# A DeltaNet and neighbourhood-attention layer: attention with unnormalised probabilities, a negated maximum, and norms of two chunks at a time

## The chip, the core and the metric

The kernel runs on one core of one Trainium2 chip. The core has five engines with a queue each: TensorE (PE, matmuls; its weight loads are listed as PEld), VectorE (DVE), ScalarE (ACT), GpSimd (POOL) and SyncE (SP, which issues the DMAs here). Each works through its queue in the order in which the program was laid out, and waits on semaphores of the others. The metric is the device time of one execution in microseconds (us), the median of the runs.

## What is computed

The layer takes 1024 latent tokens and 256 context tokens of width 1024. Half of the mixing width is a gated DeltaNet (a scan over chunks, forward and backward), half is attention: 8 heads of width 64, each latent query with one softmax over a window of latent keys and all context keys. Then come an output projection, a gated residual and a SwiGLU feed-forward part. What the change touches, cut to the core:

```python
# attention, per row block (s_win: scores of the window plus bias; s_ctx: scores of the context keys)
s = jnp.concatenate([s_win.reshape(B, H, N_COL_BLK, QB_W, n_win), s_ctx], axis=-1)
p = jax.nn.softmax(s, axis=-1).astype(v.dtype)
o = (jnp.einsum("bhnqic,binchd->bnqhd", p_win, v_r)
     + jnp.einsum("bhnqk,bkhd->bnqhd", p[..., n_win:], v_ctx))
# DeltaNet, end: sum of both directions, RMS norm per head, output gate
o = (o_f + rev(o_b)).transpose(0, 2, 1, 3)
o = rms_norm(o, out_norm_w) * jax.nn.silu(z.astype(jnp.float32))
```

## The kernel before

The kernel is one long program in stages. Input projections, short convolutions and the chunks' inverses come first. Then comes the stage of this case, in which the DeltaNet scan and the attention run side by side; after it the output projection and the feed-forward part, both almost pure matmul.

*The scan.* Ten chunks of 128 tokens (two of context, eight latent) are scanned in both directions; step `i` of the loop over `NCH` takes the i-th chunk of each direction. `scan(d, c)` is a generator: up to its first `yield` it multiplies keys by the state (L1106) and forms `vn` on DVE (L1108), then queries by the state (L1116), `y` by `vn` (L1125), the scaling `vk` on ACT (L1129), then `at` by `vn` into `oacc` (L1137, L1138) and the new state (L1142, L1148). A latent chunk that both directions have passed is finished: `finish(c)` squares it on ACT (L1163), forms an inverse root with `rsqrt`, eleven dependent steps of DVE on 128x4 numbers (L182 to L187) with three small ones around it (L1165, L1166, L1168), multiplies by it and by the gate `z` (L1170), transposes on PE (L1175) and splits the result in two parts for the output projection (L1178, L1179). From step 6 on each step finishes two chunks, one of each direction.

*The attention.* `pair(...)` handles 128 queries of two heads (`u` = 0, 1); there are 32 pairs. For each head PE forms 640 scores per query (L296) into a PSUM tile `sc` of 1536 columns, of which there are two (`bufs=2`): 640 columns for each head, and the rest, up to 1408, for the output. DVE adds the bias tile `bt` and takes the maximum in one instruction (L298, two rows in the profile: the operation and the readout of its accumulator), negates it (L300); ACT forms the exponential and its sum (L301); DVE forms the reciprocal of the sum (L302) and multiplies the 640 probabilities by it (L303). After a `yield`, PE transposes the probabilities in five blocks per head (L308), back into `sc`, and ACT copies them to `pt` (L311). After another `yield`, PE multiplies by the values (L318); the two heads use 64 columns of the array each and lie side by side. ACT copies the result into the output tile `no` (L320), and `sc` is free for the next pair but one.

*The order.* The attention is a generator too (`fill`). After each piece of the scan, `beside(PACE)` adds 0.72 to a counter, and each whole number in it advances the attention by one piece. The framework then lays the instructions of each engine out by priority and readiness, so the order in a queue isn't that of the code alone.

## Time and profile before

| what | value |
|---|---|
| median of 3 runs | 1564.35 us (1562.84 to 1565.23) |
| profiled execution | 1570.02 us, span 1568.2 us |
| mean granted TensorE clock | 0.979 |
| PE, weight loads, DVE, ACT, POOL busy | 1473.0, 1228.2, 1000.3, 721.1, 185.6 us |
| stage with scan and attention, 570 to 825 us: PE, DVE, ACT busy | 225.57, 191.87, 160.28 us of 255 |
| DMA share in this stretch | 0.78, 238 GB/s |

Busy time is a share of a stretch of time in which an engine had an instruction in work; matmuls overlap each other, so a busy PE can still have holes. In the groups by line, `x64 | 35.5, 554 | 0.5` means 64 instructions, 35.5 us busy, 554 ns each on average, and 0.5 us in which the engine was idle just before them, followed by what ended that. A 32-bit matmul shows up as two records of PE.

### The profile page before, as it was taken

Reading aid. Unit: us, or ns where it says so; the run is one execution under the profiler, and the core shown is the slowest. Engines: PE = TensorE matmul, PEld = TensorE weight load, DVE = VectorE, ACT = ScalarE, POOL = GpSimd, SP = SyncE. Lnnn points to the kernel's source line nnn. Section 1 sums busy time; section 2 is a strip of 40 time slices with the busy share of each in tenths; the row PEclk is TensorE's granted clock in tenths of the full one; section 3 lists DMA queues with packets and bytes.
Section 4 is the critical chain, followed back from the end, with each engine's and each line's share of the span. In section 5 each row is a group of like instructions: output and inputs, shape, how many; then the busy total and the mean of one; then the engine's idle time right before and its main releaser. Section 6 shows DMA issues by size and latency. Waiting matters only on the chain.

```text
span 1568.2 us, 23886 instructions
## 1 busy us (share of the span) xinstructions
PE 1473.0 (94%) x8535; PEld 1228.2 (78%) x8535; DVE 1000.3 (64%) x1877; ACT 721.1 (46%) x1406; POOL 185.6 (12%) x253
## 2 busy tenths in 40 slices
PE   3999998999999989899979989999999999999999
PEld 1789777777988868787867878888888888888887
DVE  4866479345264665678986469855555556689642
ACT  5443262684356345566753265333333334445441
POOL 1043710342043300000000000000000000000000
PEclk9999899999999999999998999999999999999999
DMA  9457133654468489899639402533323224698742
GB/s 368 132 191 229 46 85 114 218 166 144 155 217 248 154 226 307 262 287 280 199 97 303 177 29 78 194 108 116 101 101 101 101 101 146 222 369 308 236 153 82
DMA packets 214503, 280.50 MB, mean 179 GB/s; under 512 B 16288, under 2 KB 120304, under 8 KB 213360
## 3 DMA queue, kind: packets, MB, share of 16 engines
q1 hardware_dynamic: 213520, 278.34, 54.4%
q8 instruction: 67, 1.10, 0.3%
q10 hardware_dynamic: 864, 0.63, 0.1%
q14 instruction: 52, 0.43, 0.1%
HBM read 212.02 MB, written 71.08 MB: 181 GB/s over the span
## 4 chain that ended last, share of the span: by engine, by line
PE 67%; ACT 4%; DMA 4%; DVE 3%; issue 2%; POOL 1%; SPq 1%; DVEq 0%; POOLq 0%; ACTq 0%
PE ps L1232 27%; PE ps L1579 13%; PE blk L390 6%; PE ps L1363 4%; PE blk L581 3%; PE sc L318 2%; PE sc L308 2%; PE sc L296 2%; PE pr L929 2%; PE ps L1125 1%; PE ps L1385 1%; PE pr L920 1%; PE ps L1137 1%; PE ps L1142 1%; PE ps L1106 1%
## 5 line engine op out<-in xcount | busy, mean ns | idle before, releaser
L390 PE MATMUL blk<-hh,whi 128*128 128x512 f32 (+1 forms) x416 | 125.5, 396 | 9.9 <-ACT zt L592 5.7
L1293 ACT CAST uhi<-ws 128x512 fp32r<-128x512 f32 x91 | 54.8, 624 | 150.0 <-PE ps L1232 71.3
L1293 ACT CAST uhi<-wq 128x512 fp32r<-128x512 f32 x101 | 60.7, 622 | 135.6 <-issue 61.3
L390 PE MATMUL blk<-hh,wlo 128*128 128x512 f32 (+1 forms) x416 | 117.7, 379 | 2.3 <-POOL wlo L200 2.3
L390 PE MATMUL blk<-hl,whi 128*128 128x512 f32 (+1 forms) x416 | 116.4, 378 | 0.0
L1294 DVE TENSOR_TENSOR ulo<-wq,uhi 128x512 fp32r<-128x512 f32 x101 | 67.4, 688 | 66.1 <-ACT uhi L1293 36.0
L1232 PE MATMUL ps<-hT,uhi 128*128 128x512 f32 x336 | 104.6, 392 | 3.2 <-ACT hT L1411 3.1
L1232 PE MATMUL ps<-lT,uhi 128*128 128x512 f32 x336 | 103.8, 390 | 0.0
L1232 PE MATMUL ps<-hT,ulo 128*128 128x512 f32 x336 | 103.4, 389 | 0.0
L390 PEld LDWEIGHTS blk<-hh,whi 128*128 128x128 f32 x416 | 70.4, 195 | 25.6 <-ACT zt L592 6.0
L1232 PE MATMUL ps<-hB,uhi 128*128 128x512 f32 x288 | 89.7, 392 | 0.0
L390 PEld LDWEIGHTS blk<-hh,wlo 128*128 128x128 f32 x416 | 74.4, 195 | 19.3 <-POOL wlo L200 2.8
L1232 PE MATMUL ps<-lB,uhi 128*128 128x512 f32 x288 | 89.3, 391 | 0.0
L1232 PE MATMUL ps<-hB,ulo 128*128 128x512 f32 x288 | 88.8, 389 | 0.0
L581 PE MATMUL blk<-zhi,hh 128*128 128x264 f32 (+1 forms) x288 | 85.3, 296 | 0.0
L390 PEld LDWEIGHTS blk<-hl,whi 128*128 128x128 f32 x416 | 74.2, 194 | 14.1
L1294 DVE TENSOR_TENSOR ulo<-ws,uhi 128x512 fp32r<-128x512 f32 x91 | 60.8, 687 | 36.1 <-ACT uhi L1293 27.8
L581 PE MATMUL blk<-zhi,hl 128*128 128x264 f32 (+1 forms) x288 | 82.8, 287 | 0.0
L581 PE MATMUL blk<-zlo,hh 128*128 128x264 f32 (+1 forms) x288 | 82.4, 286 | 0.0
L1232 PEld LDWEIGHTS ps<-hT,uhi 128*128 128x128 f32 x336 | 63.1, 189 | 16.9 <-ACT hT L1411 3.5
L1232 PEld LDWEIGHTS ps<-lT,uhi 128*128 128x128 f32 x336 | 63.4, 189 | 13.3
L1232 PEld LDWEIGHTS ps<-hT,ulo 128*128 128x128 f32 x336 | 63.2, 188 | 13.2
(331 smaller groups left out, 3555.0 us busy)
## 6 DMA issues: line engine op xcount, KB each, us to landing
wq<-w_fo SPq DMA_DIRECT2D x99, 256.0 KB
wq<-w_gu SPq DMA_DIRECT2D x88, 256.0 KB
wad<-wa SPq DMA_DIRECT2D x64, 256.0 KB
bt<-rpb SPq DMA_DIRECT2D x64, 192.0 KB
t_d<-g SPq DMA_DIRECT2D x22, 512.0 KB
fr<-t_d SPq DMA_DIRECT2D x44, 256.0 KB
f_d<-g SPq DMA_DIRECT2D x33, 256.0 KB
fr<-f_d SPq DMA_DIRECT2D x33, 256.0 KB
```

Source lines behind the costliest of these rows:

```text
L296: pe.matmul(sc[:, u * 640 + n0:u * 640 + n1], q, ks[i], start=i == 0, stop=i == 1)
L308: pe.transpose(sc[:, u * 640 + j * 128:u * 640 + (j + 1) * 128], bt[:, j * 128:(j + 1) * 128], ident)
L318: pe.matmul(sc[u * ND:u * ND + ND, 1280:1408], vv, pt[:, j * 128:(j + 1) * 128], start=j == 0, stop=j == 4)
L390: pe.matmul(o, ww[:, k], xx[k][:, s], start=k == 0 and j == 0, stop=k == KT - 1 and j == end)
L581: pe.matmul(p[:, :c1 - c0], x[k][:, s], ww[:, k, c0:c1], start=k == 0 and j == 0, stop=k == KT - 1 and j == 2)
L920: pe.matmul(p[:, h * 128:h * 128 + 96], kk[:, h], fx[:, h, s], start=True, stop=True)
L929: pe.matmul(p[q, h * 128:h * 128 + 32 * r], f[:, h, q], y[:, h, s], start=True, stop=True)
L1232: pe.matmul(o, w[wi][:, k], x[xi][:, k], start=first and k == 0 and j == 0, stop=k == n - 1 and j == 2, skip_group_check=True)
L1293: act.copy(hi, self.raw[key])
L1294: dve.tensor_tensor(lo, self.raw[key], hi.bitcast(F32), OP.subtract)
L1363: pe.matmul(o, w[wi][:, k], parts[xi][k][:, s], start=k == 0 and j == 0, stop=k == KT - 1 and j == 2)
L1579: pe.matmul(o[b], w[wi][:, b], F[xn, p][xi], start=n in (0, 1, 5) and p == 0 and j == 0, stop=p == NFB // 2 - 1 and j == 2, skip_group_che ...
```

## The change

Four edits, all in this stage:

- The instruction at L298 now forms minus the biased score and its minimum, which is the negated maximum; the exponential takes its input times -1. The separate negation goes.
- The probabilities stay unnormalised. One reciprocal of both heads' sums (`mx[:, :, 1:2]`) replaces two, and the multiplication of the 640 probabilities goes. After the value products, two more matmuls per pair (identity times the reciprocals, repeated over 64 columns, L319 of the changed kernel) put each query's reciprocal into all 64 rows of its head, in columns 1408 to 1536 of `sc`; ACT copies them to a tile `rb` (L322) in place of its copy of the output, and DVE multiplies the output by them into `no` (L323).
- `finish` takes a list of chunks: the squares of both, one `rsqrt` on 128x8 numbers, then the rest for both.
- `finish` is no longer part of a direction's scan: chunks that end are gathered in `ended`, and a generator of its own runs for them, whose pieces advance the attention by two paces.

Lines of the changed kernel from L300 on differ from those of the kernel before: transposes L306, value products L316, norms L1170 to L1178.

On DVE, in the stretch from step 7 to step 8 of the scan, this stood in a row before (`vn` belongs to the scan):

```order
L298 ISA bt,mx<-sc,bt 128x640
L298 ISA mx 128x1
L300 TENSOR_SCALAR mx<-mx 128x1
L302 RECIPROCAL mx<-mx 128x1
L303 TENSOR_SCALAR bt<-bt,mx 128x640
L1108 SCALAR_TENSOR_TENSOR vn<-ps,EG,v 128x128 x2
L302 RECIPROCAL mx<-mx 128x1
L1108 SCALAR_TENSOR_TENSOR vn<-ps,EG,v 128x128
L303 TENSOR_SCALAR bt<-bt,mx 128x640
```

and now, at the last `vn` of the scan:

```order
L298 ISA bt,mx<-sc,bt 128x640
L298 ISA mx 128x1
L1112 SCALAR_TENSOR_TENSOR vn<-ps,EG,v 128x128 x4
L302 RECIPROCAL mx<-mx 128x2
L1112 SCALAR_TENSOR_TENSOR vn<-ps,EG,v 128x128
L323 TENSOR_TENSOR no<-sc,rb 128x8x16
```

The long multiplications and the negations are gone from between the scan's `vn`; one reciprocal and the output's multiplication, which waits for ACT, stand there instead.

On PE, behind a pair's value products, after the first half of a finish; before (`cst` is the identity, so L308 are transposes):

```order
L318 MATMUL sc<-pt,vw 64x128 x4
L318 MATMUL sc<-pt,vc 64x128
L318 MATMUL sc<-pt,vw 64x128
L318 MATMUL sc<-pt,vc 64x128
L308 MATMUL sc<-cst,bt 128x128 x5
L296 LDWEIGHTS qs
L296 MATMUL sc<-kh,qs 128x256
```

and now:

```order
L316 MATMUL sc<-pt,vw 64x128
L316 MATMUL sc<-pt,vc 64x128
L319 MATMUL sc<-cst,mx 64x128 x2
L306 MATMUL sc<-cst,bt 128x128 x5
L1185 MATMUL ps<-cst,oacc 128x128 x4
L306 MATMUL sc<-cst,bt 128x128 x5
L1185 MATMUL ps<-cst,oacc 128x128 x4
L296 LDWEIGHTS qs
```

Before, the next scores (L296) came right behind five transposes; now the two spreading matmuls follow the products, and all ten transposes and the scan's own stand before the next scores.

On DVE, the norms at the end of the stage; before (part of it):

```order
L185 TENSOR_TENSOR nwt<-orr 128x4
L1165 TENSOR_TENSOR orr<-orr,RQ_110 128x4
L186 SCALAR_TENSOR_TENSOR nwt<-nwt 128x4
L1166 TENSOR_SCALAR nwt<-orr 128x4
L187 SCALAR_TENSOR_TENSOR orr<-nwt,orr 128x4
L182 TENSOR_SCALAR nwt<-nwt 128x4
```

and now:

```order
L1170 TENSOR_TENSOR orr<-orr,RQ_110 128x4 x2
L1173 TENSOR_SCALAR nwt<-orr 128x8
L182 TENSOR_SCALAR nwt<-nwt 128x8
L183 TENSOR_SCALAR orr<-nwt 128x8
L185 TENSOR_TENSOR nwt<-orr 128x8
L186 SCALAR_TENSOR_TENSOR nwt<-nwt 128x8
L187 SCALAR_TENSOR_TENSOR orr<-nwt,orr 128x8
```

Two chunks' steps took turns; now there is one row of steps, of which each needs the one before it.

```diff
--- before.py
+++ after.py
@@ -295,13 +295,11 @@
                     for i in range(2):
                         pe.matmul(sc[:, u * 640 + n0:u * 640 + n1], q, ks[i], start=i == 0, stop=i == 1)
                 m = mx[:, u]
-                dve.tensor_tensor_reduce(bt, sc[:, u * 640:u * 640 + 640], bt, 1.0, -3.0e38, OP.add, OP.max,
+                dve.tensor_tensor_reduce(bt, sc[:, u * 640:u * 640 + 640], bt, -1.0, 3.0e38, OP.add, OP.min,
                                          m[:, 0:1])
-                dve.tensor_scalar(m[:, 1:2], m[:, 0:1], -1.0, None, op0=OP.mult)
-                act.activation(bt, bt, AF.Exp, bias=m[:, 1:2], accum_out=m[:, 2:3])
-                dve.reciprocal(m[:, 3:4], m[:, 2:3])
-                dve.tensor_scalar(bt, bt, m[:, 3:4], None, op0=OP.mult)
+                act.activation(bt, bt, AF.Exp, bias=m[:, 0:1], scale=-1.0, accum_out=m[:, 1:2])
             yield 1
+            dve.reciprocal(mx[:, :, 2:3], mx[:, :, 1:2])
             pts = []
             for u, bt in enumerate(bts):
                 for j in range(5):
@@ -317,8 +315,14 @@
                     vv = (vals[j] if w0 else vals[(j + 2) % 5])[:, u * ND:u * ND + ND]
                     pe.matmul(sc[u * ND:u * ND + ND, 1280:1408], vv, pt[:, j * 128:(j + 1) * 128],
                               start=j == 0, stop=j == 4)
-            act.copy(out.rearrange("p (r b c) -> p r b c", r=8, b=4)[:, :, cb],
-                     sc[:, 1280:1408].rearrange("p (r c) -> p r c", r=8))
+            for u in range(2):
+                pe.matmul(sc[u * ND:u * ND + ND, 1408:1536], mx[:, u, 2:3].to_broadcast([128, ND]), ident,
+                          start=True, stop=True)
+            rb = nw.tile([128, 128], F32, name="rb", tag="rb")
+            act.copy(rb, sc[:, 1408:1536])
+            dve.tensor_tensor(out.rearrange("p (r b c) -> p r b c", r=8, b=4)[:, :, cb],
+                              sc[:, 1280:1408].rearrange("p (r c) -> p r c", r=8),
+                              rb.rearrange("p (r c) -> p r c", r=8), OP.mult)
             yield 1
 
         order = [(hp, half, cb) for hp in range(NAH // 2) for half in range(2) for cb in range(4)]
@@ -1151,35 +1155,42 @@
             yield 1
             if lat:
                 if c in seen:
-                    yield from finish(c)
+                    ended.append(c)
                 seen.add(c)
 
-        def finish(c):
-            o = oacc[:, c - 2]
-            z, sq = work("z"), work("sq", 1)
-            sp.dma_start(fl(z), z_d[(c - 2) * 128:(c - 1) * 128])
-            r = sw.tile([128, 4], F32, name="orr", tag="orr")
-            for h in range(4):
-                act.activation(sq[:, h], o[:, h], AF.Square, accum_out=r[:, h:h + 1])
-            t = sw.tile([128, 3, 4], F32, name="nwt", tag="nwt")
-            dve.tensor_tensor(r, r, RQ2[:, c - 2], OP.mult)
-            dve.tensor_scalar(t[:, 0], r, 1.0 / DH, EPS, op0=OP.mult, op1=OP.add)
-            rsqrt(r, t[:, 0], t[:, 1])
-            dve.tensor_tensor(r, r, RQ[:, c - 2], OP.mult)
-            for h in range(4):
-                dve.scalar_tensor_tensor(o[:, h], o[:, h], r[:, h:h + 1], z[:, h], op0=OP.mult, op1=OP.mult)
-            yield 1
-            yield 1
-            p = bank()
-            for h in range(4):
-                pe.transpose(p[:, hs[h]], o[:, h], ident)
-            hi, lo = (x[:, :, (c - 2) * 128:(c - 1) * 128] for x in ga)
-            p = p.rearrange("p (h i) -> p h i", h=4)
-            act.activation(hi, p, AF.Copy, scale=onw)
-            dve.scalar_tensor_tensor(lo, p, onw, hi.bitcast(F32), op0=OP.mult, op1=OP.subtract)
-            yield 1
+        def finish(cs):
+            zs = []
+            r = sw.tile([128, 2, 4], F32, name="orr", tag="orr")
+            for i, c in enumerate(cs):
+                z, sq = work("z"), work("sq", 1)
+                sp.dma_start(fl(z), z_d[(c - 2) * 128:(c - 1) * 128])
+                zs.append(z)
+                for h in range(4):
+                    act.activation(sq[:, h], oacc[:, c - 2, h], AF.Square, accum_out=r[:, i, h:h + 1])
+                dve.tensor_tensor(r[:, i], r[:, i], RQ2[:, c - 2], OP.mult)
+            t = sw.tile([128, 2, 8], F32, name="nwt", tag="nwt")
+            r8 = r.rearrange("p i h -> p (i h)")
+            dve.tensor_scalar(t[:, 0], r8, 1.0 / DH, EPS, op0=OP.mult, op1=OP.add)
+            rsqrt(r8, t[:, 0], t[:, 1])
+            for i, c in enumerate(cs):
+                dve.tensor_tensor(r[:, i], r[:, i], RQ[:, c - 2], OP.mult)
+                for h in range(4):
+                    dve.scalar_tensor_tensor(oacc[:, c - 2, h], oacc[:, c - 2, h], r[:, i, h:h + 1], zs[i][:, h],
+                                             op0=OP.mult, op1=OP.mult)
+            yield 2
+            yield 2
+            for c in cs:
+                p = bank()
+                for h in range(4):
+                    pe.transpose(p[:, hs[h]], oacc[:, c - 2, h], ident)
+                hi, lo = (x[:, :, (c - 2) * 128:(c - 1) * 128] for x in ga)
+                p = p.rearrange("p (h i) -> p h i", h=4)
+                act.activation(hi, p, AF.Copy, scale=onw)
+                dve.scalar_tensor_tensor(lo, p, onw, hi.bitcast(F32), op0=OP.mult, op1=OP.subtract)
+            yield 2
 
         last = [ORDER[0][-1], ORDER[1][-1]]
+        ended = []
         count = [0.0]
 
         def beside(n):
@@ -1197,10 +1208,16 @@
             live = [scan(d, ORDER[d][i]) for d in range(2)]
             while live:
                 nxt = []
-                for n, g in enumerate(live):
-                    if next(g, 0):
+                for g in live:
+                    n = next(g, 0)
+                    if n:
                         nxt.append(g)
-                    beside(PACE)
+                    beside(PACE * max(n, 1))
+                if ended:
+                    g = finish(ended[:])
+                    ended.clear()
+                    beside(PACE * next(g))
+                    nxt.append(g)
                 live = nxt
         for _ in fill:
             pass
```

## The prediction

> **What bounds the kernel now.** I read the page first (engines, then the chain that ended last), then cut the stage that the change touches into stretches of time, then read single groups and the queue of VectorE.
>
> ```profile
> PE 1473.0 (94%) x8535; PEld 1228.2 (78%) x8535; DVE 1000.3 (64%) x1877; ACT 721.1 (46%) x1406; POOL 185.6 (12%) x253
> PE 67%; ACT 4%; DMA 4%; DVE 3%; issue 2%; POOL 1%; SPq 1%; DVEq 0%; POOLq 0%; ACTq 0%
> ```
>
> TensorE (PE) is busy for 94% of the span and carries 67% of the chain that ended last; VectorE (DVE) carries 3%. So DVE work is worth something only in a stretch where it starves PE. The change touches only the stage in which the DeltaNet scan and the attention run side by side, about 570 to 824 us. This table cuts it by what runs there; the columns are length, then busy time and instruction count of PE, weight loads, DVE, ACT and POOL, then granted clock, DMA share and GB/s.
>
> ```profile
> 590.00:613.00 23.00, 21.18 (x186) 18.66 (x182) 12.13 (x41) 12.83 (x46) 0.62 (x2) 1.00 1.05 342
> 613.00:648.00 35.00, 30.55 (x278) 25.93 (x278) 22.31 (x72) 22.01 (x54) 3.65 (x11) 0.95 0.79 247
> 648.00:670.00 22.00, 21.53 (x204) 19.09 (x203) 15.84 (x50) 14.02 (x37) 1.87 (x6) 1.00 0.91 276
> 670.00:691.00 21.00, 20.79 (x198) 18.43 (x196) 15.43 (x50) 13.28 (x36) 1.56 (x5) 1.00 0.90 274
> 691.00:713.00 22.00, 20.37 (x195) 18.09 (x195) 16.91 (x57) 11.86 (x31) 2.22 (x6) 1.00 0.99 294
> 713.00:735.00 22.00, 19.24 (x173) 16.23 (x174) 18.36 (x79) 13.85 (x41) 1.87 (x6) 0.92 0.94 277
> 735.00:748.00 13.00, 12.15 (x122) 10.84 (x122) 11.29 (x38) 8.39 (x21) 1.25 (x4) 1.00 0.91 277
> 750.00:767.00 17.00, 15.14 (x135) 11.91 (x136) 16.24 (x74) 11.86 (x35) 1.87 (x6) 1.00 0.70 209
> 767.00:781.00 14.00, 13.99 (x145) 12.41 (x146) 12.79 (x43) 9.94 (x26) 1.72 (x4) 1.00 0.59 184
> 783.00:799.00 16.00, 14.22 (x129) 11.28 (x127) 15.46 (x70) 11.07 (x32) 1.87 (x6) 1.00 0.47 147
> 799.00:810.00 11.00, 10.92 (x111) 9.75 (x110) 9.90 (x36) 6.38 (x14) 0.00 (x0) 1.00 0.08 24
> ```
>
> The recorded busy time of PE contains the latency of each matmul, so I count matmul records per us instead. Three kinds of stretch show. (1) Up to 713, the two long even stretches (648 to 691) run 402 records in 43 us, 9.3 per us, with DVE at 73% and DMA at 0.9; before them, 613 to 648 runs 7.9 per us with DVE at 64%: DVE isn't what is short there. (2) The stretches 713-735, 750-767 and 783-799, in which finished chunks are normalised (I call them the finish stretches), run 437 records in 55 us, 7.9 per us, with DVE busy for 50.06 of 55 us (91%). (3) The stretches between them, 735-748, 767-781 and 799-810, run 378 records in 38 us, 9.95 per us. So PE is starved by DVE in 55 us of the kernel, and nowhere else for long.
>
> **The change part by part.**
>
> ```profile
> L298 DVE CUSTOM_DVE_ANT_0 bt<-sc,bt 128x640 f32<-128x640 f32 x64 | 52.5, 822 | 22.6 <-PE sc L296 10.7 <-POOL bt L264 4.6 <-DMA bt<-rpb 3.7
> L303 DVE TENSOR_SCALAR bt<-bt,mx 128x640 f32<-128x640 f32 x64 | 35.5, 554 | 0.5
> L302 DVE RECIPROCAL mx<-mx 128x1 f32<-128x1 f32 x64 | 10.2, 159 | 8.8 <-ACT bt L301 8.1
> L300 DVE TENSOR_SCALAR mx<-mx 128x1 f32<-128x1 f32 x64 | 9.2, 147 | 0.5
> L1131 DVE TENSOR_TENSOR vn<-ps,NB 128x512 f32<-128x512 f32 x16 | 11.0, 688 | 5.5 <-ACT vk L1129 5.0 <-PE ps L1125 0.3
> L185 DVE TENSOR_TENSOR nwt<-orr 128x4 f32<-128x4 f32 x24 | 3.8, 158 | 0.1
> L320 ACT COPY no<-sc 128x128 f32<-128x128 f32 x32 | 8.5, 266 | 16.3 <-PE sc L318 16.0
> 772.23 1.24 PE sc L318 x20
> 713.00:735.00 22.00, 2.87 (x6) 0.92 0.94 277
> 750.00:767.00 17.00, 2.75 (x5) 1.00 0.70 209
> 783.00:799.00 16.00, 2.38 (x5) 1.00 0.47 147
> ```
>
> The last three rows are the stretches again, with only the probabilities' multiplication (L303) counted.
>
> *DVE, per pair of heads.* Removed: two multiplications, two reciprocals, two negations, 2 x (0.554 + 0.159 + 0.147) = 1.72 us. Added: one reciprocal of two columns, 0.16 us by L302, and one multiplication of 128x128 from PSUM: between L185 (4 columns, 0.158) and L1131 (512 columns, 0.688) a straight line gives 0.29. Net 1.27 us less; over 32 pairs 41 us of DVE. The finish stretches hold 16 such multiplications, 8 pairs, so 10 us of their 50.
>
> *ACT.* The exponential takes a constant factor and the same bias, and the copy of the output becomes an equal copy of the spread reciprocals: 0.266 us out, 0.266 in. Nothing.
>
> *PE.* Two matmuls per pair are added, in the same shape and the same side-by-side placing as the value products. Those are 20 records in 1.24 us (the row above, from the chain), 0.062 each; the two new ones make 4 records, 0.25 us. Over 32 pairs 8 us. Nothing hides work of PE where PE is the bound. The bounds are 0.25 us a pair and nothing (a pair in a hole of PE).
>
> *The finish stretches.* If DVE isn't short any more, PE can run their 437 records at the neighbours' 9.95 per us: 43.9 us, and 8 x 0.25 = 2.0 for the new matmuls, 45.9 instead of 55. DVE would need 50 - 10 = 40 us there, so PE sets it. That is -9.1 at best; at worst nothing, if ACT holds PE instead. I take -7.5, near the upper end, because the neighbours reach their rate with DVE still 89% busy. One of these stretches also holds a half clock:
>
> ```profile
> 725.70:729.10 3.40, 3.27 (x20) 2.94 (x22) 2.88 (x21) 1.98 (x5) 0.62 (x2) 0.50 0.83 197
> ```
>
> It follows a hole of PE behind DVE and costs about 1.7 us of the 9.1.
>
> *The rest after 713* (38 us, 7 pairs): 7 x 0.25 = +1.75 of PE at worst, nothing at best; DVE gets shorter by 8.9 of 34 us. I take +1.
>
> *Before 713* (33 multiplications of the 64, 16.5 pairs): +4.1 if all of it shows. In 590 to 648 the DMA share (1.05) and the low rate leave holes for half of it, and each head's chain of scores, maximum, exponential, transposes loses the negation, the reciprocal and the multiplication, 0.86 us, ahead of the transposes, which also frees the bias buffers earlier. Bounds -3 and +4.1; I take +0.5.
>
> *The score buffer.* Two buffers of scores exist. Before, the buffer went free after the value products and a 0.266 us copy; now after the products, the spread, the copy, a hop to DVE and 0.29 us. The order of PE allows for it: before, in 15 of 32 pairs at most the five transposes of one head stood between a pair's last product and the next scores on PE; now in 6. Each of these 6 would wait about 0.4 us longer (0.29, and 0.1 that I allow for the hop), +2.4; against that the waits of before go:
>
> ```profile
> PE sc L296 <- ACT no L320: 2.0, 6, 0.4
> ```
>
> I take +0.5, bounds -2 and +4. Behind the waiting scores stand the scan's matmuls on PE, so such a wait delays both.
>
> *The norms of two chunks in one.* Here the count of instructions misleads. These are the norms at the end of the stage, first one chunk alone, then both mixed:
>
> ```profile
> 814.97 0.16 DVE L1165 TENSOR_TENSOR orr<-orr,RQ 128x4 f32<-128x4 f32 x1 [0.45 <-ACT sq L1163]
> 815.17 0.17 DVE L1166 TENSOR_SCALAR nwt<-orr 128x4 f32<-128x4 f32 x1
> ...
> 816.45 0.15 DVE L1165 TENSOR_TENSOR orr<-orr,RQ 128x4 f32<-128x4 f32 x1
> 816.57 0.16 DVE L186 SCALAR_TENSOR_TENSOR nwt<-nwt 128x4 f32<-128x4 f32 x1
> 816.65 0.16 DVE L1166 TENSOR_SCALAR nwt<-orr 128x4 f32<-128x4 f32 x1
> ...
> 820.17 1.14 DVE L1170 SCALAR_TENSOR_TENSOR oacc<-oacc,orr,z 128x128 f32<-128x128 f32 x4
> ...
> 820.67 1.17 PE L1175 MATMUL ps<-cst,oacc 128*128 128x128 f32 x4 [1.25 <-DVE oacc L1170]
> ```
>
> A step that needs the one before it starts 0.20 us after it; steps of two chunks in turn start 0.10 apart. Twice twelve steps in turn take 2.4 us, and twelve merged steps that wait for each other take 2.4 too. So I price the merge at 0 (best: -1.2 per finish, where other work of DVE fills the gaps). At the end of the stage it is no gain: now all eight multiplications wait for the second chunk's squares; from 816.45 come 0.2 for that step, 2.4, 0.3 for two small products and eight multiplications at 1.14 for four, so the last one ends near 821.6, where before it ended at 821.3. I take +0.3 (bounds -1.2 and +1.5).
>
> The Trainium skill, page "VectorE: DVE Perf Modes", section "Rules for kernel authors", says that chained operations gain nothing from tricks between them and that only the count of operations matters. By that rule a merge would save 12 x 0.16 = 1.9 us each of the four times, 7.7 in all, and the sum would be near 1551; the rows above go against it where two chains alternate.
>
> *Sum*: -7.5 + 1 + 0.5 + 0.5 + 0 + 0.3 = -5.2 us. The profiled execution took 1570.02 us (span 1568.2); the sum makes it 1564.8. The median of the runs is 1564.35, 0.36% below the profiled one; the same 5.2 us from it give 1559.2.
>
> **The rivals.**
>
> *More than that.* DVE relief shows everywhere: the finish stretches give all 9.1, the rest after 713 gives 1 instead of costing 1, the part before 713 gives 2, the release costs nothing, the tail gives 1.2: -13.3, 1551. For it: DVE is 89% busy in the stretches between, too. Against: they run at the highest rate of the stage already.
>
> *No change.* PE pays for what DVE gains. ACT has 36.8 us in the 55 us of the finish stretches, and the largest waits of PE in the stage are for ACT's copies of the transposed probabilities, which the change keeps:
>
> ```profile
> PEld sc L318 <- ACT pt L311: 7.2, 18, 1.1
> PEld sc L308 <- ACT pt L311: 5.7, 13, 1.5
> ```
>
> If these hold half of the finish stretches' gain, 3.7 us, the sum is -1.5: 1562.9.
>
> *Slower.* The output's multiplication stands in DVE's queue behind a maximum of the next pair (0.822 and its 0.08 readout) that was issued earlier; the scores of the pair after next wait for it on PE, with the scan behind them. If that happens, a release comes 0.4 + 0.9 = 1.3 us late. It decides where less than that stands between: about 12 pairs, 12 x 0.9 = +10.8 in place of my +0.5, sum +5: 1569.5. Against: the order of PE was laid out around it. That it happens in fewer than 6 pairs would make it harmless. The Trainium skill, page "PSUM — Partial Sum Buffer", section "Engine vs sequencer instructions", calls these queues strictly first in, first out, which speaks for this rival; no row of before shows this multiplication.
>
> **How the numbers follow.** Chances: my forecast (2 to 9 us gained) 0.47, more than that 0.13, no change 0.23, slower 0.17. A measurement of this kernel tells about 0.2%, 3.1 us, from no change. Faster by more: 0.13 and nearly all of the forecast's, 0.42, together 0.55; within: 0.23 and the rest of the forecast, 0.28; slower 0.17. The range goes from 1551 (the first rival) to 1569 (just short of the last); the forecast alone would be 1555 to 1562.
>
> **What would show it.** Right: the finish stretches get shorter by 6 to 8 us together at 9.5 or more records per us; DVE falls by about 40 us in the stage; the new matmuls take 0.25 us a pair; the last transposes of the stage come no earlier behind the end of the scan than now. Wrong: PE waits for the output's multiplication with more than 4 us in total (the slower rival); the finish stretches keep their length while PE waits for the copies L311 (no change); the part before 713 moves by more than 4 us either way, since there I only guess how holes and added matmuls meet.

## The result, and the profile after

The changed kernel takes 1567.76 us (median of 11 runs) where the kernel before, in the same job, takes 1564.35 us: a ratio of 1.0027, 95% interval 1.0015 to 1.0040. A second job, reported below, gave 1.0008 (0.9996 to 1.0021). So the change costs about 1 or about 4 us, by the job; the second can't be told from no change by itself. The prediction was 1559.2 us, a gain of 5.2.

The page of the profiled execution (1565.93 us), its busy times and the shares of the chain that ended last:

```profile
PE 1478.5 (95%) x8663; PEld 1233.2 (79%) x8663; DVE 968.6 (62%) x1701; ACT 721.1 (46%) x1406; POOL 185.4 (12%) x253
PE 75%; DMA 10%; ACT 5%; DVE 4%; POOL 3%; issue 2%; SPq 1%; ACTq 0%; POOLq 0%; DVEq 0%
```

DVE has 32 us less, PE 128 matmul records more, ACT the same. This single profile is 4 us shorter than the one that the prediction started from, against the medians; so both kernels were profiled again, and the stage is read from these. Four stretches each, cut at the scan's matmuls `at` x `vn` (L1137 before, L1141 after): from the first scores to the first of them (step 2), to step 6 (the first step that finishes chunks), to the last step, and to the first matmul of the output projection. Columns as in the prediction's table. The kernel before, profiled again:

```profile
573.90:613.70 39.80, 31.82 (x264) 26.73 (x263) 22.34 (x66) 24.26 (x64) 1.87 (x6) 0.91 0.95 296
613.70:710.30 96.60, 91.95 (x870) 80.56 (x869) 70.73 (x230) 61.34 (x157) 9.28 (x28) 1.00 0.92 278
710.30:806.60 96.30, 88.89 (x842) 75.32 (x842) 87.10 (x341) 64.48 (x174) 8.57 (x26) 1.00 0.67 199
806.60:819.60 13.00, 5.73 (x46) 4.31 (x45) 9.34 (x41) 5.49 (x22) 0.00 (x0) 0.81 0.31 109
```

The changed kernel, first profile:

```profile
573.20:614.90 41.70, 34.55 (x281) 28.65 (x281) 19.51 (x53) 25.43 (x67) 1.87 (x6) 0.92 0.91 281
614.90:711.40 96.50, 95.38 (x917) 83.30 (x916) 57.11 (x169) 60.95 (x153) 8.74 (x28) 1.00 0.93 277
711.40:809.90 98.50, 95.35 (x926) 80.29 (x925) 73.45 (x250) 64.68 (x177) 8.12 (x26) 1.00 0.69 200
809.90:821.50 11.60, 4.23 (x24) 3.27 (x25) 8.11 (x29) 4.76 (x20) 0.00 (x0) 0.67 0.29 94
```

And its second profile:

```profile
572.10:616.10 44.00, 35.89 (x281) 30.28 (x281) 19.52 (x53) 25.49 (x67) 1.87 (x6) 0.88 0.84 265
616.10:713.10 97.00, 95.37 (x918) 83.37 (x917) 57.12 (x169) 60.93 (x154) 8.72 (x28) 1.00 0.94 278
713.10:811.50 98.40, 95.25 (x925) 80.28 (x924) 73.40 (x250) 64.58 (x177) 8.09 (x26) 1.00 0.67 198
811.50:823.20 11.70, 4.32 (x25) 3.37 (x25) 8.16 (x29) 4.82 (x20) 0.00 (x0) 0.70 0.29 98
```

The stage takes 245.7 us before, 248.3 and 251.1 after: +1.9 and +4.2 ahead of step 2 (the second profile has one half clock more there, a piece of time with a granted clock of 0.50, 3.4 us long), -0.1 and +0.4 up to step 6, +2.2 and +2.1 in the steps that finish chunks, -1.4 and -1.3 at the end. The third stretch holds 84 records of PE more, about 60 of the spreading and some 20 that stood in the fourth before, so the last two are best read together: +0.8 both times. The place where the prediction saw its gain has not become shorter, although DVE fell from 87.1 of 96.3 us (90%) to 73.45 of 98.5 (75%).

The first profile of before, from which the prediction argued, had a stage of 250.1 us. The 4.4 us more lie at two places, each with a half clock that the second profile doesn't have: step 2 to 3 took 35.5 us there and 31.8 here, step 6 to 7 35.4 and 34.2. The latter is the half clock from which the prediction took 1.7 of its 9.1 us.

What the two new operations cost on PE can be read at any pair that has no wait behind it. Before, the last value product and what follows on PE:

```profile
796.48 0.27 PE L318 MATMUL sc<-pt,vc 128*64 128x128 f32 x1
796.68 0.94 PE L1106 MATMUL ps<-s,kT 128*128 128x128 f32 x6
```

After, with the copy on ACT and the multiplication on DVE:

```profile
802.39 0.27 PE L316 MATMUL sc<-pt,vc 128*64 128x128 f32 x1
802.50 0.39 PE L319 MATMUL sc<-cst,mx 128*64 128x128 f32 x4
802.82 0.77 PE L306 MATMUL sc<-cst,bt 128*128 128x128 f32 x5
...
802.93 0.27 ACT L322 COPY rb<-sc 128x128 f32<-128x128 f32 x1 [0.49 <-PE sc L319]
...
803.23 0.29 DVE L323 TENSOR_TENSOR no<-sc,rb 128x128 f32<-128x128 f32 x1 [0.34 <-ACT rb L322]
```

From the last product's start to the next operation 0.20 us before and 0.43 after; over all 32 pairs the medians are 0.20 and 0.42. So the spreading costs PE 0.22 us a pair, 7.0 us in all. The score buffer goes free 1.07 us behind the last product here (from 802.39, plus 0.06 for the product itself, to 803.52); the mean over the 32 pairs is 1.48 us, before it was 0.77. The multiplication itself takes 0.29 us, as priced.

### The profile page after: what moved, and what is told of

It reads as the page before. It is cut to its first block, busy times and chain, and to the rows that moved or that the text cites. A ratio compares the mean times of both kernels' runs of the same rounds, so it can differ in the third digit from the quotient of the medians.

```text
span 1564.2 us, 23860 instructions
## 1 busy us (share of the span) xinstructions
PE 1478.5 (95%) x8663; PEld 1233.2 (79%) x8663; DVE 968.6 (62%) x1701; ACT 721.1 (46%) x1406; POOL 185.4 (12%) x253
## 4 chain that ended last, share of the span: by engine, by line
PE 75%; DMA 10%; ACT 5%; DVE 4%; POOL 3%; issue 2%; SPq 1%; ACTq 0%; POOLq 0%; DVEq 0%
PE ps L1249 26%; PE ps L1596 13%; PE blk L394 11%; PE ps L1380 4%; PE sc L316 3%; PE blk L585 2%; PE sc L306 2%; PE sc L296 2%; PE pr L933 2%; DMA nv_d<-zt 1%; DMA wraw<-w_conv 1%; PE ps L1129 1%; PE ps L1110 1%; PE pr L924 1%; PE ps L1146 1%
```

## The experiments

All ratios are to the kernel before in the same job; five rounds each (9 to 12 runs, where nothing else is said).

**Both kernels once more**, to know what one profile is worth.

> The kernel before, once more, as a yardstick. Its profiled execution took 1570.02 us, 5.7 over the median of its runs, and its stage (first scores L296 to first L1363) 250.1 us, 1.8 more than the 248.3 of the changed kernel, which by its runs is 4.2 us slower. If that one profile was an outlier, the stage takes 243 to 247 us here and the ratio is within 0.15% of 1. If the loss of the change lies outside the stage, the stage takes 250 again.

Ratio 1.0002 (0.9987 to 1.0017), stage 245.7 us: the first profile of before was the outlier.

> The changed kernel, once more. The first profile's stage took 248.3 us. If the loss of 0.27% lies in the stage, the stage takes 248 to 251 us here and stays at least 2 us above that of the kernel before in the same job; if it lies elsewhere, the two stages are alike or this one is shorter, and the loss shows as half clocks in the 740 us behind it. Ratio 1.001 to 1.004 by either.

1.0008 (0.9996 to 1.0021), stage 251.1 us. Both profiles say that what the change costs lies in the stage: outside it they are 1.5 and 2.1 us shorter than the second one of before.

**Each half of the change alone.** The attention's edits with the old `finish`, and the merged `finish` with the old attention; each is one part of the diff above, unchanged.

> The attention's edits alone (negated maximum in one step, unnormalised probabilities, spread reciprocals, output multiplied on DVE); the norms as before. Theory 1 (PE pays 0.25 us a pair for the spreading and DVE's relief buys nothing back, because the scan's chain of dependent steps, not DVE, sets the finish stretches): +4 to +8 us, ratio 1.002 to 1.005. Theory 2 (the loss comes from the merged finish, which gives the attention 15 paces a step where it had 14 and leaves the end of the stage without cover): -2 to -6 us, ratio 0.996 to 0.999. The prediction's terms without the merge: -5.5 us.

1.0032 (1.0018 to 1.0047), +5.0 us, the worst of the three. Its profile, the four stretches:

```profile
569.90:611.60 41.70, 33.55 (x280) 27.76 (x280) 19.43 (x53) 25.25 (x67) 1.87 (x6) 0.96 0.90 282
611.60:709.10 97.50, 95.45 (x919) 83.44 (x917) 57.10 (x169) 61.01 (x154) 8.72 (x28) 1.00 0.94 274
709.10:809.90 100.80, 95.29 (x926) 80.57 (x925) 75.51 (x285) 63.71 (x176) 8.09 (x26) 1.00 0.65 192
809.90:821.50 11.60, 4.38 (x26) 3.31 (x24) 8.93 (x41) 4.98 (x20) 0.00 (x0) 0.76 0.36 123
```

> The merged finish alone, with its generator and its paces; the attention as before. Theory 1: within 0.1% of the kernel before. Theory 2: +4 to +8 us, ratio 1.002 to 1.005, with the attention's last value products 4 us or more ahead of the scan's last at x vn and a longer hole of PE behind. The prediction's price: +0.3 us.

1.0017 (1.0005 to 1.0028), +2.7 us. The last two stretches of its profile:

```profile
707.90:807.30 99.40, 90.48 (x861) 76.25 (x861) 84.43 (x306) 64.23 (x175) 9.08 (x26) 1.00 0.66 197
807.30:818.90 11.60, 4.24 (x25) 3.29 (x25) 8.12 (x29) 4.77 (x20) 0.00 (x0) 0.68 0.30 105
```

The attention's last product comes 4.6 us ahead of the last `at` x `vn` (1.5 before), which is the lead that theory 2 named, without its +4 to +8 us. The third stretch also holds 19 records more; +3.1 and -1.4 us. Alone the merge costs; on top of the attention's edits it doesn't (1.0032 without it, 1.0008 and 1.0027 with it). The halves don't add. This kernel has the merged norms and the separate generator with its paces, so the two aren't told apart.

**The negated maximum alone.**

```diff
-dve.tensor_tensor_reduce(bt, sc[...], bt, 1.0, -3.0e38, OP.add, OP.max, m[:, 0:1])
-dve.tensor_scalar(m[:, 1:2], m[:, 0:1], -1.0, None, op0=OP.mult)
-act.activation(bt, bt, AF.Exp, bias=m[:, 1:2], accum_out=m[:, 2:3])
+dve.tensor_tensor_reduce(bt, sc[...], bt, -1.0, 3.0e38, OP.add, OP.min, m[:, 0:1])
+act.activation(bt, bt, AF.Exp, bias=m[:, 0:1], scale=-1.0, accum_out=m[:, 2:3])
```

> The negated maximum alone: 64 instructions of 0.147 us less on DVE, nothing else. If DVE's relief in steps 6 to 9 is worth what the prediction took (7.5 us for 10 of 50 us), the 16 negations there (2.4 us) give -1.7 us, ratio 0.998 to 0.9995; if relief is worth nothing, ratio 0.9995 to 1.0005.

0.9998 (0.9986 to 1.0010): nothing, 64 instructions of DVE less. Its profile shows how little one stage length proves. The stage is 250.2 us, 4.5 more than in the second profile of before, although the runs are alike; the third stretch has a half clock of 6.8 us:

```profile
709.30:810.30 101.00, 92.35 (x858) 78.64 (x856) 85.48 (x313) 63.59 (x174) 8.59 (x26) 0.97 0.66 193
```

**The relief without its price, and the price without the relief.** First the attention's edits without `reciprocal`, L319, L322 and L323; this kernel leaves the normalisation out, so it is a measure of time and not a layer:

```diff
-dve.reciprocal(mx[:, :, 2:3], mx[:, :, 1:2])
...
-for u in range(2): pe.matmul(sc[...], mx[:, u, 2:3].to_broadcast([128, ND]), ident, ...)
-rb = ...; act.copy(rb, sc[:, 1408:1536]); dve.tensor_tensor(out, sc[:, 1280:1408], rb, OP.mult)
+act.copy(out, sc[:, 1280:1408])
```

> The attention's edits alone, norms as before, and the normalisation left out: no reciprocal, no spreading matmuls, no output multiplication; ACT copies the output as before. So DVE has all of its relief (1.72 us a pair) and PE has the work of before. The prediction's step (relief lets PE run the finish stretches at the neighbours' rate, 7.5 us or more, and something elsewhere): stage 234 to 239 us against 245.7 before, ratio 0.993 to 0.997. Theory 3 (relief is worth nothing or little, the holes of PE that DVE seemed to end are the latency of a pair's own chain and of ACT's copies): stage 243 to 247 us, ratio 0.998 to 1.0005.

0.9962 (0.9945 to 0.9979), -5.9 us by the runs, stage 242.2 us (-3.5):

```profile
572.50:613.60 41.10, 33.52 (x265) 27.73 (x265) 17.45 (x45) 24.08 (x65) 1.88 (x6) 0.92 0.91 282
613.60:707.70 94.10, 93.00 (x877) 81.50 (x877) 52.89 (x145) 62.52 (x159) 8.74 (x28) 1.00 0.94 281
707.70:803.00 95.30, 88.45 (x854) 75.45 (x853) 70.20 (x255) 63.67 (x173) 8.12 (x26) 1.00 0.69 207
803.00:814.70 11.70, 4.42 (x27) 3.21 (x25) 8.66 (x40) 5.05 (x21) 0.00 (x0) 0.80 0.35 122
```

By the runs this lies in the range that the prediction's step had (0.993 to 0.997); the stage lies between the two forecasts, nearer that of theory 3. Where the other 2.4 us are wasn't found. With all of the relief and nothing to pay, the steps that finish chunks and the end become 2.3 us shorter (96.3 + 13.0 to 95.3 + 11.7). The prediction's step, without the 2.0 us that it charged for the spreading, gives 55 - 43.9 = 11.1 at best.

Then the kernel before with the spreading added, its result not read:

```diff
+for u in range(2):
+    pe.matmul(sc[u * ND:u * ND + ND, 1408:1536], mx[:, u, 3:4].to_broadcast([128, ND]), ident, ...)
 act.copy(out..., sc[:, 1280:1408]...)
```

> The kernel before with the two spreading matmuls of each pair added and their result not read: 128 records of PE, 8 us, nothing else. Theory 1 (PE is the bound in the stage; the diagonal's kernel paid 24.6 us for 35.7 us of added work): +5 to +8 us, ratio 1.003 to 1.005. Rival (the holes of PE take the added work in): +0 to +2 us, ratio 0.9995 to 1.0015.

1.0029 (1.0013 to 1.0044), +4.5 us (2.0 to 6.9) for 7.0 us of PE: more paid than not, between the two forecasts. The stage of its one profile, 251.9 us, is no measure of that, for a half clock of 6.8 us lies in its third stretch too:

```profile
707.40:809.40 102.00, 94.33 (x925) 81.79 (x924) 87.47 (x342) 64.99 (x175) 8.41 (x26) 0.97 0.62 183
```

**Half of ACT's copies to DVE**, in the kernel without normalisation.

```diff
-act.copy(pt, sc[:, u * 640:u * 640 + 640])
+(dve.tensor_copy if u else act.copy)(pt, sc[:, u * 640:u * 640 + 640])
```

> The kernel without normalisation (no reciprocals, no spread; 0.9962), with the second head's copy of the transposed probabilities (L309, 32 copies of 128x640) on DVE instead of ACT. Theory 6 (PE's holes in the finish stretches are waits for ACT's copies in ACT's queue): holes of PE there fall by 3 us or more, stage 236 to 240 us against 242.2, ratio 0.991 to 0.995. Rival (the holes are the latency of each pair's chain in PE's fixed order, whoever copies): stage 241 to 244, ratio 0.995 to 0.998.

0.9954 (0.9938 to 0.9970; 6 runs), stage 242.1 against 242.2 us. The third stretch:

```profile
701.80:797.00 95.20, 89.11 (x864) 76.32 (x863) 79.70 (x272) 55.22 (x158) 8.10 (x26) 1.00 0.70 205
```

ACT has 8.5 us less, DVE 9.5 more, and the stretch is as long as without this edit. Theory 6 finds no support, and neither the amount of DVE's work nor of ACT's seems to hold these steps; that the two shifts cancel isn't excluded.

**The diagonal instead of the spread.** `dg` = identity times reciprocals (128x128, DVE); the transposes become matmuls by it.

```diff
-pe.transpose(sc[...], bt[:, j * 128:(j + 1) * 128], ident)
+pe.matmul(sc[...], bt[:, j * 128:(j + 1) * 128], dg, start=True, stop=True)
```

> Unnormalised probabilities and negated maximum, the norms as before, but the reciprocals are not spread: DVE multiplies the identity (128x128) by them per head, and the transposes multiply by this diagonal instead of by the identity, so the normalisation costs PE nothing and the output is copied by ACT as before. DVE keeps 1.1 us of its 1.27 us a pair. Theory 1 (the spreading's 128 records, 8 us of PE, ate what DVE's relief gave; relief is worth 2 to 5 us): stage 241 to 244 us against 245.7 before and 251.6 with the spreading; ratio 0.996 to 0.999. Theory 3 (the relief is worth nothing, because PE waits for ACT's copies of the transposed probabilities whatever DVE does): stage 245 to 247, ratio 0.9995 to 1.001.

1.0147 (1.0130 to 1.0163; 4 runs), stage 270.3 us.

> The same diagonal with the merged finish. Theory 1: 8 us under the changed kernel in PE's work, stage 241 to 245 us, ratio 0.996 to 0.999. Theory 3: stage 246 to 248, ratio 1.000 to 1.001. If the merge costs by itself (the finish alone stood 0.17% above before), this is 1 to 3 us above the diagonal with the norms as before; if it is worth something only when DVE is relieved (the steps 6 to 9 and the tail took 110.1 us with both edits, 112.6 with the attention's alone, 111.0 with the finish's alone, 109.3 before), it is 1 to 3 us below it.

1.0160 (1.0144 to 1.0175; 4 runs). Both expectations missed one thing, which the groups show; the kernel before, then the diagonal's:

```profile
L308 PE MATMUL sc<-cst,bt 128*128 128x128 f32 x320 | 48.9, 284 | 4.1 <-ACT pt L311 2.7 <-DVE nwt L182 0.8
```

```profile
L308 PE MATMUL sc<-dg,bt 128*128 128x128 f32 x640 | 88.6, 285 | 1.1 <-ACT pt L311 0.8
```

A 32-bit transpose by the identity is one record, a 32-bit matmul of the same shape two. 320 records more, at the 0.12 us by which such records follow each other (802.82 to 803.42 for five, above), are 38 us of PE; the stage paid 24.6. As a test of theories 1 and 3 the two runs are void; as a price they say that the stage pays about 0.65 us for each us of work added to PE, with what DVE's relief gives already taken off.

**The loads ahead of the scan.** SP's queue around the scan's first loads, before:

```profile
582.56 0.35 SPq L265 DMA_DIRECT2D bt<-rpb  x1
582.96 0.56 SPq L1079 DMA_DIRECT2D kT<-kT_d  x1
```

and in the changed kernel, with what the last but one waited for:

```profile
580.62 1.01 SPq L265 DMA_DIRECT2D bt<-rpb  x2
584.31 0.38 SPq L271 DMA_DIRECT2D vw<-vw_d  x1
584.74 0.57 SPq L1083 DMA_DIRECT2D kT<-kT_d  x1
...
SPq L271 <- PE sc L316: 2.6, 1, 2.6
```

A second bias tile and a `vw` have moved ahead of the scan's loads, which start 11.5 us behind the first scores instead of 9.1. Four buffers of `vw` were to take the wait away:

```diff
-vw = nw.tile([128, 3, 128], F32, name="vw", tag="vw", bufs=3)
+vw = nw.tile([128, 3, 128], F32, name="vw", tag="vw", bufs=4)
```

> The changed kernel with four buffers of the window's values vw instead of three. In the changed kernel the fourth pair's vw stands in SP's queue ahead of the scan's first loads and waits 2.6 us there for a pair's value products; before, one bias tile stood there alone. Theory 4 (the 2 to 4 us that the changed kernel loses before the first at x vn, 41.7 and 44.0 us behind the first scores against 39.8, come from this wait): the wait goes, the first at x vn comes 39.5 to 40.5 us behind the first scores, ratio 1.000 to 1.001. Rival (the DMA engines, 84 to 90% busy there, set the start of the scan, or the added matmuls do): 41.5 to 44 us again, ratio as for the changed kernel.

1.0003 (0.9991 to 1.0014), but not by theory 4: the wait is still there, for a `vw` of a later pair (the prefetch runs as far ahead as it has buffers), and the scan's loads start at 11.7 us:

```profile
SPq L271 <- PE sc L316: 2.7, 1, 2.7
```

What the order of the loads costs wasn't shown by this run. In the other profiles the first `at` x `vn` comes 39.3 to 40.3 us behind the first scores where no `vw` stands ahead (before twice, the merge alone, the added spread, and one of the kernels below that spread early) and 40.5 to 42.0 where one does (nine profiles, besides the one at 44.0 and one at 43.4, which have a half clock more each). But the negated maximum alone (41.7) and the other kernel that spreads early (41.1) have no `vw` ahead either, only a longer half clock. So it is 1 us at most, and not shown.

**The release of the score buffer.** Attention's edits, with one edit more:

```diff
-act.copy(rb, sc[:, 1408:1536])
-dve.tensor_tensor(out, sc[:, 1280:1408], rb, OP.mult)
+act.copy(rb, sc[:, 1280:1536])                       # rb is 128x256 now
+dve.tensor_tensor(out, rb[:, 0:128], rb[:, 128:256], OP.mult)
```

> The attention's edits alone (1.0032), but ACT copies the output and the spread reciprocals in one copy of 256 columns, which frees the score buffer; DVE multiplies afterwards from SBUF. The work is the same but for 128 more columns of ACT's copy. Theory 5 (the release of the buffer by DVE, 0.6 us later a pair, costs about 5 of the 10.9 us between the kernel without normalisation and this): last product to free falls from 1.37 to about 1.0 us, stage from 251.6 to 247 to 249 us, ratio 1.000 to 1.002. Rival (PE's added work alone does it): stage and ratio as for the attention's edits, 1.003 to 1.004.

1.0001 (0.9991 to 1.0011) against 1.0032, stage 247.1 against 251.6:

```profile
573.70:615.00 41.30, 34.38 (x276) 28.64 (x276) 18.60 (x51) 24.75 (x64) 1.87 (x6) 0.92 0.91 286
615.00:712.40 97.40, 96.15 (x922) 84.26 (x920) 57.70 (x171) 63.07 (x157) 8.72 (x28) 1.00 0.95 272
712.40:809.10 96.70, 92.37 (x926) 79.79 (x924) 75.72 (x285) 65.10 (x176) 8.09 (x26) 1.00 0.70 202
809.10:820.80 11.70, 4.43 (x27) 3.34 (x25) 8.94 (x41) 5.16 (x21) 0.00 (x0) 0.74 0.35 119
```

Nearly all of it lies in the third stretch, 96.7 us against 100.8 for the same 926 records. From the last product to the free buffer it is 1.18 us on the mean (1.37 without the edit), and to the scores of the pair after next 1.98 us (2.30; before 1.51). But without the edit PE has no wait for this release in the third stretch at all, and 0.4 us in the whole stage, so the 4.1 us don't show as such waits.

> The changed kernel with one edit: ACT copies the output and the spread reciprocals together (256 columns) and so frees the score buffer; DVE multiplies afterwards from SBUF. With the attention's edits alone this gave 4.8 us. Theory 5: 2 to 5 us under the changed kernel (1.0008 and 1.0027), ratio 0.998 to 1.0005, holes of PE in the stage 48 to 51 us against 52.5 and 55.4. Rival (the merged finish had already taken up what the release cost): ratio 1.0005 to 1.002.

1.0013 (0.9999 to 1.0028), stage 247.9 us: no better than the changed kernel (1.0008, 1.0027; 248.3, 251.1). So the edit gains with the old `finish`, and nothing that can be measured with the merged one; theory 5 does not explain the changed kernel.

**Cheaper spreads.** The reciprocals written 64 times per head (`rw`, 128x128) and one transpose for two matmuls, with four `vw` buffers (first two runs), taken ahead of the value products and copied along with the probabilities (next two), or with the early release (last):

```diff
-dve.reciprocal(mx[:, :, 2:3], mx[:, :, 1:2])
+dve.reciprocal(rw, mx[:, :, 1:2].to_broadcast([128, 2, ND]))
...
-for u in range(2): pe.matmul(sc[...], mx[:, u, 2:3].to_broadcast([128, ND]), ident, ...)
+pe.transpose(sc[:, 1408:1536], rw.rearrange("p a b -> p (a b)"), ident)
```

> The attention's edits with a cheaper spread, four buffers of vw, norms as before: the reciprocal is written 64 times per head (128x128) and spread by one transpose of 128 columns (one record of 0.12 us a pair) instead of two matmuls (four records of 0.062). 4 us of PE less. Theory 1: 3 to 5 us under the attention's edits alone (ratio 1.0032 then), another 1 to 2 from vw: ratio 0.9985 to 1.0005. If PE's work doesn't set the stage: 1.001 to 1.003.

1.0015 (1.0002 to 1.0028).

> The changed kernel with the one transpose in place of the two spreading matmuls and four buffers of vw. The changed kernel with the buffers alone had 1.0003. Theory 1: 3 to 4 us less, ratio 0.9975 to 0.999. If PE's work doesn't set the stage: 1.000.

1.0006 (0.9993 to 1.0020).

> Attention's edits with the spread taken ahead: one transpose of the reciprocals (128x128) behind the second head's transposes, into the columns next to its probabilities, so that ACT's copy of these takes it along (768 columns instead of 640, and no copy of its own); behind the value products only DVE's multiplication is left. Norms as before. Theory 5: last product to free 0.5 to 0.7 us where DVE is not busy with a maximum, stage 242 to 246 us, ratio 0.996 to 0.9995. If the release doesn't matter: PE's work 4 us over the kernel before, relief 3 to 6: ratio 0.9995 to 1.001. If DVE's queue holds the multiplication behind maxima (the prediction's slower rival): last product to free above 1.2 us on the mean and ratio above 1.001.

1.0010 (0.9997 to 1.0023), last product to free 0.81 us (0.77 before).

> The same with the merged finish and its paces. With the changed kernel's attention the merge was worth 1 to 3 us (1.0032 alone, 1.0008 and 1.0027 with both): ratio 0.9955 to 0.999 by theory 5. If the merge is worth nothing or costs as it did alone (+2.6 us): 1 to 3 us above the run before this.

1.0008 (0.9997 to 1.0019).

> The attention's edits with the early release and with the spread by one transpose a pair (0.12 us of PE instead of 0.25), norms as before. With the release alone 1.0001. Theory 1 (PE's work counts): 2 to 4 us less, ratio 0.9975 to 0.999, faster than both kernels. If the transposed spread gives nothing (its kernels without the early release stood at 1.0015 and 1.0006): 1.000.

1.0012 (1.0000 to 1.0024). None is faster than before, all five miss the range that theory 1 or 5 gave them, and the last does not improve on the early release alone (1.0001). Two prices that I had taken from rows of other shapes were wrong. The transpose costs PE 0.17 us a pair, not 0.12 (0.37 us from the last product to the next operation, median of 32 pairs, against 0.42 with two matmuls); and the reciprocal, in the group of the last kernel:

```profile
L303 DVE RECIPROCAL rw<-mx 128x128 f32<-128x128 f32 x32 | 30.4, 949 | 7.5 <-ACT bt L300 7.2
```

0.95 us instead of 0.16: 25 us of DVE given away for 1.6 us of PE. A narrow reciprocal with a broadcast copy behind it wasn't tried.

## Why the prediction was wrong, step by step

*The step that failed: "If DVE isn't short any more, PE can run their 437 records at the neighbours' 9.95 per us".* DVE was 91% busy, but PE wasn't starved by it. What ended PE's idle time in the third stretch (total us, times, longest), in the second profile of before:

```profile
PE sc L318 <- ACT pt L311: 2.6, 5, 0.9
PE sc L296 <- ACT no L320: 1.6, 5, 0.4
PE sc L308 <- ACT pt L311: 1.1, 1, 1.1
PE sc L308 <- DVE nwt L182: 0.8, 1, 0.8
PE sc L296 <- DVE mx L298: 0.5, 1, 0.5
```

PE was idle for 7.4 of 96.3 us, and DVE ended 1.3 of them. Each row names the last releaser only, so what DVE delayed further back in the chain isn't in it; the kernel without the normalisation is the firmer evidence. With the relief and nothing to pay it was idle for 6.9 of 95.3 us, and the rows of that kernel (transposes L305) name other releasers:

```profile
PE sc L296 <- DVE mx L298: 2.0, 2, 1.1
PE sc L305 <- DVE nwt L186: 1.6, 2, 0.8
PE sc L296 <- ACT no L317: 1.1, 3, 0.4
PE sc L305 <- DVE mx L298: 1.1, 2, 0.7
```

So the holes stayed as long. PE ran 854 records there at 9.0 per us with DVE at 74%, with ACT relieved too 9.1; before 8.7. The term of -7.5, which is -9.5 without the spreading, measured -2.3 us (end included); 1.2 of the difference is the half clock that the second profile of before doesn't have. By the runs all of the relief, wherever it acts, is worth 5.9 us (3.3 to 8.6). What holds PE there instead was not settled: a pair's chain of scores, maximum, exponential, transposes, copy, in the fixed order of PE's queue, is what is left, and that is argued only. The copies L311, which the rival of no change named, ended 3.7 of the 7.4 us, but moving half of them to DVE gained nothing.

*The relief itself.* Priced as durations, 1.27 us a pair, 41 us. DVE's busy time in the stage fell by 28.5 us with the attention's edits (189.5 to 161.0 us over the four stretches, sums of the rows above): small instructions overlap. The 64 negations, 9.4 us as durations, took 4.7 us of busy time with them when they went alone (189.5 to 184.8). Two rows of the second profile of before show it, where the next instruction starts 0.07 us behind a negation of 0.15 us:

```profile
796.36 0.15 DVE L300 TENSOR_SCALAR mx<-mx 128x1 f32<-128x1 f32 x1
796.43 0.15 DVE L302 RECIPROCAL mx<-mx 128x1 f32<-128x1 f32 x1
```

*PE: the size was right, its way into the sum wrong.* 0.25 us a pair predicted, 0.22 measured. But of its 8 us the sum let only 3.5 show (2.0 in the finish stretches, 1, 0.5), and alone it cost 4.5 us. By the runs the pieces are relief -5.9 and spread +4.5, together -1.4. The attention's edits measured +0.2 with the early release and +5.0 without, the changed kernel +1.2 and +4.2, each figure with 2 to 3 us of uncertainty. So the spreading takes back most of what the relief gives; the rest of the loss, 2.6 to 5.6 us in the changed kernel, these pieces do not explain, and its cause stays open. In the stage, by single profiles: behind step 6 the prediction had -5.7 (the release and the end included), the relief alone measured -2.3 and the changed kernel +0.8 both times, so the relief's term, 7.2 us too large (-9.5 for -2.3), is about the miss of 6.5 there; ahead of it the prediction had +0.5 (bounds -3 to +4.1), the relief alone measured -1.2 and the changed kernel +1.8 and +4.6, the latter with one half clock more.

*The slower rival had the right side for the wrong reason.* Its multiplication does not stand behind maxima: it starts 0.14 us behind its copy on the mean, over 0.5 us in 2 of 32 pairs, and PE's waits for it come to 0.6 us in both profiles, where the prediction's sign was 4 us. The Trainium skill, page "PSUM — Partial Sum Buffer", section "Engine vs sequencer instructions", has the queues strictly first in, first out; no row here speaks against it, but the order laid out leaves the room, as the prediction's argument against the rival had it.

*The release*, taken at +0.5 (bounds -2 to +4): as a wait of PE it fell from 2.0 us (the copy, before) to 0.6. With the old finish the early release was worth 4.8 us by the ratios, with the merged one nothing that can be measured, as the prediction had it for the changed kernel. Each edit lays PE's queue out anew, and how much of the 4.8 us is the release and how much a luckier order stays open; PE's waits of 0.4 us for the release speak for the order.

*The merge*, taken at 0 (end +0.3): the end is as forecast, the last transposes L1175 and L1185 start 7.9 us behind the scan's last `at` x `vn` in both kernels. The merged steps start 0.20 us apart, as priced. But alone the merge, with its generator and paces, cost 2.7 us (0.8 to 4.4), by the ratio outside its bounds (-1.2 to +1.5); why was not found. The Trainium skill's rule on page "VectorE: DVE Perf Modes", section "Rules for kernel authors", that the count of operations decides, would have given 7.7 us by the prediction's estimate; the runs show nothing of that, and for these chains the row of alternating steps was the better guide.

*What no step had:* the queue of SP. In the changed kernel a second bias tile and a `vw` stand ahead of the scan's first loads; that the buffers which go free earlier, counted as a help, let them move there is likely, but not shown, and neither is a cost.

## What to carry to other kernels

A busy share of 91% shows that an engine works, not that another starves for it: first read which engine ends the other's idle time (DVE ended 1.3 of 7.4 us here), then leave the work out in an experiment, and pay for its removal only when that shows the gain. Where PE is nearly always busy, an exchange of DVE's time for PE's must be counted near PE's whole price (4.5 of 7.0 us here), and pieces that are measured alone need not add up. A profile of one execution carries half clocks that others don't have (4.4 us of stage in the first profile of before); before a few us are read from one stretch, take a second.

## What the runs showed of the hardware that I had not expected

- A 32-bit matmul of 128x128 by 128x128 appears as two records, a 32-bit transpose as one (640 against 320 records for the same ten blocks a pair): +24.6 us of stage.
- A reciprocal on DVE takes 0.163 us for 2 columns and 0.949 us for 128, where a multiplication of 128 columns takes 0.289.
- Two matmuls of 64 columns of the array, side by side behind others of their kind, cost PE 0.22 us, one full transpose behind them 0.17 (medians of 32 pairs).
